# Three buffers for gathered rows and an earlier lead for gathers, in a mixture-of-experts layer

## The chip, the core and the metric

The kernel runs on one core of a Trainium2 chip. A core has five engines, each with its own instruction stream: TensorE (PE in the profile, with its weight loads apart as PEld), VectorE (DVE), ScalarE (ACT), GpSimd (POOL) and SyncE (SP). DMA transfers are issued by an engine into a queue and run beside the engines. The metric is the device time of one execution in microseconds (us); the figure given is the median of several runs.

## What is computed

One layer of a hybrid model over 1024 tokens of width 1024, in float32: a state-space mixer and a windowed attention in parallel, an output projection, a mixture of 32 experts, and a final norm. Only the expert stage matters here. In the reference it is (cut):

```
def hier_moe(h, w_group, b_group, w_expert, b_expert, w_gate, w_up, w_down):
    ...            # top-1 of 4 groups, then top-2 of its 8 experts; weights per token
    order = jnp.argsort(flat_e)
    ...            # assignments sorted by expert into blocks of 128, each of one expert
    x_buf = h_pad[tok_buf].reshape(n_blocks, MOE_BLOCK, d)
    def expert_block(args):
        xb, e = args
        return (jax.nn.silu(xb @ w_gate[e]) * (xb @ w_up[e])) @ w_down[e]
    y_buf = lax.map(expert_block, (x_buf, blk_e)).reshape(n_slots, d)
    out = jax.ops.segment_sum(y_buf.astype(f32) * w_buf[:, None], tok_buf, num_segments=n_tok + 1)
```

`w_gate` and `w_up` are 1024 x 512 for each expert, `w_down` is 512 x 1024: 6 MB of weights per expert, all of which must be read.

## The kernel before

**Blocks.** The expert stage (`moe`) walks 33 blocks, one for each place in a list of experts, and one more for the second part of the expert at place 13 (`MID`). The order is 0 to 13, then block 32 (`NE`), then 14 to 31. Fifteen places (`HALVES`: 3, 4, 6, 8, 10, 12, 14, 16, 18, 20, 22, 24, 27, 29, 31) and block 32 are half blocks, with up to 64 tokens; below they carry an h (block 10h). The others are full blocks of up to 128 tokens. An expert whose tokens don't fit is finished in `moe_rest`, a loop over overflow blocks near 990 us.

**One block.** A table in device memory, `tab`, holds for each block its token numbers, its output rows and its weights.
- `lst_load` brings a block's table entries into `lst` (DMAs on SP's queue, L1198: one for a full block, two for a half block, since the 64 entries are laid down twice). For a half block it then makes the half-row numbers `hrow` with one VectorE instruction (L1200): 64 tokens by two half rows of 512.
- `gather` issues an indirect DMA on POOL's queue that fetches the block's rows from `h2d` into `xe` (L1236 with `lst`, 128 x 1024; L1231 with `hrow`, 128 x 512, which fills half of the buffer only). There are two `xe` buffers, used in turn.
- `x_t` (L1306) or `half_x` (L1249) transposes the rows on PE into `pxe`; ScalarE and VectorE copy them out.
- `gu` (L1319) or `half_gu` (L1260) multiplies by the gate and up weights into `pgu`, the activation follows, and `down` (L1345) or `half_down` (L1284) multiplies by the down weights into `py`.
- `y_out` (L1351, tile `ye`) or `half_y` (L1289, `yeh`, in the same two buffers) weighs the result on VectorE.
- `y_add` (L1355) or `half_add` (L1293) issues an indirect DMA on POOL's queue that adds the rows of `ye` to `acc` in device memory.

**Weights.** 192 loads of 1 MB (tile `wf`, L1215, on SP's queue) go through 13 slots. For full blocks ScalarE (L179, `wh`) and VectorE (L180, `wl`) split them into a high and a low part; half blocks use them as they are.

**Order.** `schedule` lists the steps; behind the third quarter of block p's gate and up matmuls stands a step ("x", p), at which `x_ahead` transposes the next block, issues the gather of the block two behind that one, and has loaded the entries two blocks before the gather. The instructions of each engine are then put into a fixed order by a scheduler at build time, and every engine works through its order; POOL issues gathers and adds in one row, so an instruction that waits holds up all behind it.

Of the kernel before, what the change touches and what calls it, by code (L numbers as in the profile page):

```python
# [17 lines left out]
P = 128  # L18
# [7 lines left out]
NE = 32  # L26
# [12 lines left out]
OOB = 1 << 20  # L39

NR, NL, NW = 7, 6, 4

NCH = 6

# [80 lines left out]
class Kern:  # L125
# [1049 lines left out]

    def moe_bufs(self):
        nc = self.nc
        self.xe = [self.mp([D], "xe%d" % k) for k in range(2)]
        for t in self.xe:
            nc.gpsimd.memset(t, 0.0)  # L1180
        self.lst = self.mp([NE + 1, 4], "lst", 1, I32)
        self.hrow = self.mp([NE + 1], "hrow", 1, I32)
        self.EV = {}
# [5 lines left out]
    def lst_load(self, b):  # L1189


        nc = self.nc
        e = self.expert_at(MID if b == NE else b)
        r, n = P if b == NE else 0, H if self.half(b) else P
        tv = self.tab.rearrange("(e r) c -> e r c", e=NE)[:, r:r + n, :]
        src = tv[e] if isinstance(e, int) else tv[bass.ds(e, 1)].rearrange("o r c -> (o r) c")
        for p in range(0, P, n):
            nc.sync.dma_start(out=self.lst[p:p + n, b, :], in_=src)  # L1198
        if self.half(b):
            nc.vector.tensor_scalar(self.hrow[:, b:b + 1], self.lst[:, b, 0:1], 2.0, self.C[:, C_HALF:C_HALF + 1], op0=OP.mult, op1=OP.add)  # L1200

    def side(self):

# [25 lines left out]
    def gather(self, k, lst, b=None):  # L1229
        if b is not None and self.half(b):  # L1230
            self.nc.gpsimd.indirect_dma_start(  # L1231
                out=self.xe[k % 2][:, 0:D // 2], out_offset=None, in_=self.h2d.rearrange("t (a c) -> (t a) c", a=2),
                in_offset=bass.IndirectOffsetOnAxis(ap=self.hrow[:, b:b + 1], axis=0),
                bounds_check=2 * NT - 1, oob_is_err=False)
            return
        self.nc.gpsimd.indirect_dma_start(  # L1236
            out=self.xe[k % 2], out_offset=None, in_=self.h2d[:, :],
            in_offset=bass.IndirectOffsetOnAxis(ap=lst[:, 0:1], axis=0),
            bounds_check=NT - 1, oob_is_err=False)


    def half_x(self, k):

        nc = self.nc
        xv = self.xe[k % 2][:, 0:D // 2].rearrange("s (p i) -> s i p", i=4)
        xT = self.mp([4, P], "xT", 2, tag="xh", size=D)
        ps = self.bank([4, P], name="pxe")
        for i in range(4):
            nc.tensor.transpose(ps[:, i, :], xv[:, i, :], self.ident)  # L1249
        nc.scalar.copy(xT, ps)  # L1250
        return xT
# [45 lines left out]

    def x_t(self, e, out=None, ps=None):
        nc = self.nc
        xv = self.xe[e % 2].rearrange("s (a p i) -> s a i p", a=2, i=4)  # L1300
        xh, xl = out or (self.mp([8, P], "xh", 2, F32R), self.mp([8, P], "xl", 2, F32R))
        fixed = ps
        for h in range(2):
            ps = self.bank([4, P], name="pxe") if fixed is None else fixed
            for k in range(4):
                nc.tensor.transpose(ps[:, k, :], xv[:, h, k, :], self.ident)  # L1306
            s = slice(4 * h, 4 * h + 4)
            nc.scalar.copy(xh[:, s, :], ps)
            nc.vector.tensor_tensor(xl[:, s, :], ps, xh[:, s, :].bitcast(F32), OP.subtract)
        return xh, xl  # L1310
# [138 lines left out]
    def moe(self):  # L1449
        blocks = list(range(MID + 1)) + [NE] + list(range(MID + 1, NE))  # L1450
        at = lambda p: [p, NE] if p == MID else [p]
        X, A, T, Y, Z, G = {}, {}, {}, {}, {}, {}
        done = 0
        add = lambda b: self.half_add(Z.pop(b), b) if self.half(b) else self.y_add(Z.pop(b), self.lst[:, b, :])

        def x_ahead(p):

            nonlocal done
            for b in at(p):
                k = blocks.index(b)  # L1460
                X[b] = self.half_x(k) if self.half(b) else self.x_t(k)
                for i in range(done, min(k + 3, NE + 1)):
                    if 4 <= i + 2 < NE + 1:
                        self.lst_load(blocks[i + 2])
                    self.gather(i, self.lst[:, blocks[i], :], blocks[i])
                done = min(k + 3, NE + 1)

        for i in range(3):
            self.lst_load(i)
        for i in range(2):  # L1470
            self.gather(i, self.lst[:, i, :])
        self.g2 = self.mod_load(self.mp, 3, "g2")
        self.g2h = self.mp([512], "g2h")
        for n in range(2):
            self.nc.sync.dma_start(out=self.g2h[n * H:n * H + H], in_=self.modd[3][None, n * 512:n * 512 + 512].to_broadcast([H, 512]))
        self.counts()
        self.lst_load(3)
        done = 2
        x_ahead(0)
        for t in self.steps:  # L1480
            k, p = t[0], t[-1] if len(t) == 2 else t[1] if len(t) > 2 else None
            if k == "gu":
                if t[2] == 0:
                    for b in at(p):
                        G[b] = self.bank2(name="pgu")
                wg, wu = self.parts_for(p, (2 * t[2], 2 * t[2] + 1), (0, 0, 2, NW)[t[2]])
                for b in at(p):
                    if self.half(b):
                        self.half_gu(t[2], X[b], *((wg, wu) if self.half(p) else (wg[2], wu[2])), G[b])
                    else:  # L1490
                        self.gu(t[2], X[b], wg, wu, G[b])
            elif k == "act":
                for b in at(p):
                    A[b] = (self.half_act if self.half(b) else self.act)(G.pop(b))
            elif k == "x":
                if p + 1 < NE:
                    x_ahead(p + 1)
            elif k == "hT":
                for b in at(p):
                    T[b] = (self.half_h if self.half(b) else self.h_t)(A.pop(b))  # L1500
                    Y[b] = self.bank2(name="py")
            elif k == "down":
                w, = self.parts_for(p, (8 + t[2],), 0)
                for b in at(p):
                    if self.half(b):
                        self.half_down(T[b], w if self.half(p) else w[2], Y[b], t[2])
                    else:
                        self.down(T[b], w, Y[b], t[2])
            elif k == "y":
                for b in at(p):  # L1510
                    Z[b] = self.half_y(Y.pop(b), b) if self.half(b) else self.y_out(Y.pop(b), self.lst[:, b, :])
                    if p != REST - 1:
                        add(b)
            elif k == "rest":
                self.moe_rest()
                self.rested = True
                for b in list(Z):
                    add(b)
            elif k == "final":
                self.final()  # L1520
            elif k == "last":
                self.final_rows(Y.pop(p))
# [63 lines left out]
    def final(self):  # L1586

        nc = self.nc
        self.nf = self.mp([D], "nf", 2, tag="xl")
        nc.scalar.dma_start(out=self.nf, in_=self.a["norm_final"].to_broadcast([P, D]))  # L1590
        self.nfh, self.pair = self.mp([D // 2], "nfh", 2, tag="xh", size=D), self.mp([P], "pair")
        for n in range(2):
            nc.scalar.dma_start(out=self.nfh[n * H:n * H + H], in_=self.a["norm_final"][:, n * 512:n * 512 + 512].to_broadcast([H, 512]))

            nc.vector.tensor_tensor(self.pair[:, n * H:n * H + H], self.ident[:, 0:H], self.ident[:, H:P], OP.add)
        hr = self.mp([1], "hr", 1, I32)
        nc.vector.tensor_scalar(hr, self.lst[:, NE - 1, 1:2], 2.0, self.C[:, C_HALF:C_HALF + 1], op0=OP.mult, op1=OP.add)
        self.rowsy = self.mp([D // 2], "ya", 2, tag="xl", size=D)
        nc.gpsimd.indirect_dma_start(
            out=self.rowsy, out_offset=None, in_=self.acc.rearrange("t (a c) -> (t a) c", a=2),  # L1600
            in_offset=bass.IndirectOffsetOnAxis(ap=hr[:, 0:1], axis=0),
            bounds_check=2 * (NT + P) - 1, oob_is_err=False)
        ys = [self.mp([D], "yf", NW, tag=("wh", "wl")[b % 2]) for b in range(NBX)]
        for b in range(NBX):
            nc.sync.dma_start(out=ys[b], in_=self.acc[b * P:(b + 1) * P, :])
        self.ys = ys
# [165 lines left out]
```

## Time and profile before

| | us |
|---|---|
| median of 3 runs | 1357.1 (1354.55 to 1357.25) |
| profiled execution, time | 1359.11 |
| its span | 1357.3 |
| PE busy | 1167.5 (86%) |
| DVE, ACT, POOL busy | 829.9, 599.3, 337.4 |
| first gather of the expert stage issued | 693.45 |
| last add of the expert stage issued | 1316.70 |

The profile comes from one execution of its own, recorded by the hardware. A row of the timeline gives the start, the length, the engine, the source line, the operation, "out<-in" by tile names, the count of instructions in the row (x3) and, in brackets, how long the engine sat idle ahead of it and what released it. "issue" there means that it waited for nothing that the profile shows. Waits are listed as total us, times, longest us. A window's row gives the busy time of each engine, the granted PE clock (1.00 is full), the busy share of the 16 DMA engines (which can exceed 1 a little) and GB/s.

### The profile page before, as it was taken

The numbers are of one execution on the slowest core, as the hardware profiler recorded it, in microseconds if no ns is written. First come the engines' busy times: TensorE is split into PE (matmuls) and PEld (weight loads), VectorE is DVE, ScalarE is ACT, GpSimd is POOL, SyncE is SP. The second block draws the span as 40 slices with busy tenths as digits, with TensorE's granted clock in tenths as the row PEclk, the third lists the DMA queues.
The fourth block names the chain that finished last, engine by engine and source line by source line (L and its number), as shares of the span: only waits on it lengthen the run. The fifth ranks groups of instructions, "written<-read, shape, count | busy, mean of one in ns | idle before, by whom it ended". The sixth has DMA issues, their size and how long they took to land. (4 is left out here: it accounts for less than half of the span.)

```text
span 1357.3 us, 18757 instructions
## 1 busy us (share of the span) xinstructions
PE 1167.5 (86%) x6630; PEld 859.6 (63%) x6630; DVE 829.9 (61%) x1399; ACT 599.3 (44%) x1064; POOL 337.4 (25%) x290
## 2 busy tenths in 40 slices
PE   5799999888888999899938999697999968989981
PEld 2588778788876666687726666454556645566550
DVE  1688984788848877556678544353456535466533
ACT  4633322455367766433436434333244423354323
POOL 0340001577623444022331121111121211102110
PEclk9789999989888999999969899798999979989996
DMA  9755645766223300873467899999589999989846
GB/s 330 266 200 163 209 139 157 250 204 202 96 77 120 109 9 16 293 265 124 165 235 262 312 371 406 374 353 361 206 322 402 404 376 319 343 327 355 334 154 263
DMA packets 104512, 335.02 MB, mean 247 GB/s; under 512 B 19562, under 2 KB 37994, under 8 KB 79840
## 3 DMA queue, kind: packets, MB, share of 16 engines
q1 hardware_dynamic: 94672, 314.78, 62.4%
q0 software_dynamic: 9008, 17.10, 5.3%
q10 hardware_dynamic: 736, 1.92, 0.4%
q8 instruction: 53, 0.87, 0.3%
q14 instruction: 43, 0.35, 0.1%
HBM read 299.74 MB, written 43.43 MB: 253 GB/s over the span
## 5 line engine op out<-in xcount | busy, mean ns | idle before, releaser
L180 DVE TENSOR_TENSOR wl<-wf,wh 128x1024 fp32r<-128x1024 f32 x204 | 242.0, 1221 | 118.8 <-ACT wh L179 118.3
L179 ACT CAST wh<-wf 128x1024 fp32r<-128x1024 f32 x204 | 205.1, 1051 | 175.3 <-PE pgu L1319 140.2
L1260 PE MATMUL pgu<-wf,xT 128*64 128x256 f32 x1024 | 130.6, 386 | 0.4 <-DVE yeh L1289 0.4
L1319 PE MATMUL pgu<-wl,xh 128*128 128x512 f32 x272 | 95.3, 418 | 12.7 <-DVE wl L180 12.5
L1260 PEld LDWEIGHTS pgu<-wf,xT 128*64 128x64 f32 x1024 | 71.9, 137 | 47.9 <-issue 12.6
L1319 PE MATMUL pgu<-wh,xh 128*128 128x512 f32 x272 | 97.6, 432 | 4.4 <-ACT wh L179 4.4
L466 PE MATMUL pzq<-xw,hxh 128*128 128x256 f32 x512 | 100.2, 295 | 0.0
L768 POOL TENSOR_SCALAR p<-p,sst 128x640 f32<-128x640 f32 (+1 forms) x32 | 66.1, 2065 | 103.9 <-DVE sst L765 53.7
L1355 POOL DMA_INDIRECT acc<-ye,lst x17 | 33.5, 1972 | 234.4 <-DVE ye L1351 164.2
L1319 PE MATMUL pgu<-wh,xl 128*128 128x512 f32 x272 | 89.0, 407 | 0.0
L1345 PE MATMUL py<-wh,hT 128*128 128x512 f32 x272 | 81.9, 410 | 2.3 <-ACT hT L1337 2.3
L466 PEld LDWEIGHTS pzq<-xw,hxh 128*128 128x128 f32 x512 | 83.1, 197 | 1.0 <-issue 0.2
L347 PE MATMUL pxb<-hxh,xw 128*128 128x512 f32 x256 | 76.4, 397 | 0.0
L1319 PEld LDWEIGHTS pgu<-wl,xh 128*128 128x128 f32 x272 | 53.8, 198 | 32.6 <-DVE wl L180 20.2
L466 PE MATMUL pzq<-xw,hxl 128*128 128x256 f32 x256 | 74.3, 290 | 0.0
L1319 PEld LDWEIGHTS pgu<-wh,xh 128*128 128x128 f32 x272 | 52.0, 201 | 34.2 <-ACT wh L179 18.8
L1306 PE MATMUL pxe<-C,xe 128*128 128x128 f32 x136 | 26.5, 332 | 51.9 <-DMA xe<-h2d,lst 49.2
L1293 POOL DMA_INDIRECT acc<-yeh,hrow x15 | 32.8, 2185 | 153.8 <-DVE yeh L1289 136.9
L751 DVE TENSOR_REDUCE sst<-psc 128x1 f32<-128x640 f32 (+1 forms) x64 | 50.4, 789 | 29.7 <-PE psc L750 24.7
L1284 PE MATMUL py<-wf,hTh 128*64 128x512 f32 x256 | 64.1, 622 | 0.5 <-ACT hTh L1277 0.5
L1345 PEld LDWEIGHTS py<-wh,hT 128*128 128x128 f32 x272 | 50.3, 193 | 20.4 <-issue 5.3
L1319 PEld LDWEIGHTS pgu<-wh,xl 128*128 128x128 f32 x272 | 53.6, 197 | 14.3 <-issue 3.2
(352 smaller groups left out, 2528.6 us busy)
## 6 DMA issues: line engine op xcount, KB each, us to landing
wf<-in_w_gate SPq DMA_DIRECT2D x64, 1024.0 KB, 14.1
wf<-in_w_up SPq DMA_DIRECT2D x64, 1024.0 KB, 8.7
wf<-in_w_down SPq DMA_DIRECT2D x64, 1024.0 KB, 13.2
wa<-in_w_ada SPq DMA_DIRECT2D x48, 512.0 KB, 4.7
R<-csd SPq DMA_DIRECT2D x16, 512.0 KB, 4.7
xl<-xd SPq DMA_DIRECT2D x17, 256.0 KB, 3.4
xt<-in_x SPq DMA_DIRECT2D x8, 512.0 KB, 7.9
xf<-in_w_xbc SPq DMA_DIRECT2D x8, 512.0 KB, 4.3
```

The lines of the kernel that those rows point to most:

```text
L179: self.nc.scalar.copy(hi, src)
L180: (eng or self.nc.vector).tensor_tensor(lo, src, hi.bitcast(F32), OP.subtract)
L347: nc.tensor.matmul(px[s], w(wp, kc), self.hx(hp, kc, s, 512), start=st, stop=sp)
L466: nc.tensor.matmul(ps, self.hx(hp, kc, b // 4, P, (b % 4) * P), w(wp, kc), start=kc == 0 and hp + wp == 0, stop=kc == KC - 1 and hp == 1)
L751: v.tensor_reduce(mx, ps[:, o:512 + nl], AX.X, OP.max)
L768: (v if j % 2 else nc.gpsimd).tensor_scalar(p_, p_, den[:, j - i:j - i + 1], None, op0=OP.mult)
L1260: self.nc.tensor.matmul(pg[n * H:n * H + H, o:o + 256], xT[:, i0 + kk, a * H:a * H + H], w[:, kk * 512 + n * 256:kk * 512 + n * 256 + 256] ...
L1284: self.nc.tensor.matmul(py[n * H:n * H + H, 0:512], hT[:, i, a * H:a * H + H], w[:, n * 512:n * 512 + 512], start=f == 0, stop=f == 3)
L1293: self.nc.gpsimd.indirect_dma_start(out=self.acc.rearrange("t (a c) -> (t a) c", a=2), out_offset=bass.IndirectOffsetOnAxis(ap=self.hrow[: ...
L1319: nc.tensor.matmul(pg[:, n * 512:(n + 1) * 512], x[xp][:, k, :], w[wp][:, kk * 512:(kk + 1) * 512], start=k == 0 and xp + wp == 0, stop=k ...
L1345: nc.tensor.matmul(py[:, n * 512:(n + 1) * 512], hT[:, hp, f, :], wd[wp][:, n * 512:(n + 1) * 512], start=f == 0 and hp + wp == 0, stop=f ...
L1355: self.nc.gpsimd.indirect_dma_start(out=self.acc[:, :], out_offset=bass.IndirectOffsetOnAxis(ap=lst[:, 0:1], axis=0), in_=y, in_offset=Non ...
```

## The change

A third `xe` buffer is added (`NX`), with its memset. `x_ahead` for the block at place k now issues gathers up to place k+3 (it was k+2), makes half-row numbers up to place k+4, and loads table entries up to place k+6. At the start three gathers and seven blocks' entries are issued (two and four before). Making half-row numbers is split from `lst_load` into `half_rows`. The small tile `pair`, used at the end, shares the buffers of `hT`. Core of the diff (`% 2` became `% len(self.xe)` in `gather`, `half_x` and `x_t` too):

```diff
+NX, TABLE_AHEAD = 3, 3
...
-        self.xe = [self.mp([D], "xe%d" % k) for k in range(2)]
+        self.xe = [self.mp([D], "xe%d" % k) for k in range(NX)]
...
+    def half_rows(self, b):
         if self.half(b):
-            nc.vector.tensor_scalar(self.hrow[:, b:b + 1], ...)
+            self.nc.vector.tensor_scalar(self.hrow[:, b:b + 1], ...)
...
-        done = 0
+        done = rows = tabs = 0
...
         def x_ahead(p):
-            nonlocal done
             for b in at(p):
                 k = blocks.index(b)
                 X[b] = self.half_x(k) if self.half(b) else self.x_t(k)
-                for i in range(done, min(k + 3, NE + 1)):
-                    if 4 <= i + 2 < NE + 1:
-                        self.lst_load(blocks[i + 2])
-                    self.gather(i, self.lst[:, blocks[i], :], blocks[i])
-                done = min(k + 3, NE + 1)
-
-        for i in range(3):
-            self.lst_load(i)
-        for i in range(2):
-            self.gather(i, self.lst[:, i, :])
+                rows_to(k + NX + 1)
+                gather_to(k + NX + 1)
+                rows_to(k + NX + 2)
+                tables_to(k + NX + 1 + TABLE_AHEAD)
+
+        def gather_to(n):
+            nonlocal done
+            for i in range(done, min(n, NE + 1)):
+                self.gather(i, self.lst[:, blocks[i], :], blocks[i])
+                done = i + 1
...
+        def tables_to(n):
+            nonlocal tabs
+            for i in range(tabs, min(n, NE + 1)):
+                self.lst_load(blocks[i])
+                tabs = i + 1
+
+        tables_to(FIXED)
+        gather_to(FIXED)
...
-        self.lst_load(3)
-        done = 2
+        tables_to(NX + 1 + TABLE_AHEAD)
         x_ahead(0)
...
-        self.nfh, self.pair = self.mp([D // 2], "nfh", 2, tag="xh", size=D), self.mp([P], "pair")
+        self.nfh, self.pair = self.mp([D // 2], "nfh", 2, tag="xh", size=D), self.mp([P], "pair", 2, tag="hT", size=D)
```

`rows_to` is the same loop over `half_rows`; `FIXED` is 3. In the new kernel the lines of the block functions stand 2 to 4 further down: gathers are L1240 and L1235, transposes L1310 and L1253, adds L1359 and L1297, gate and up matmuls L1323 and L1264, `yeh` L1293.

What this does to the orders is shown at two places. First POOL's order before, from the gather of block 7 to that of block 11. `xe_6889` and `xe_6890` are the two buffers; the gathers are of blocks 7, 8h, 9, 10h and 11, and the adds of blocks 4h, 5, 6h and 7:

```order
L1236 DMA xe_6890<-h2d,lst 128x1024
L1293 DMA acc<-yeh,hrow 2304x512
L1231 DMA xe_6889<-h2d,hrow 128x512
L1355 DMA acc<-ye,lst 1152x1024
L1236 DMA xe_6890<-h2d,lst 128x1024
L1231 DMA xe_6889<-h2d,hrow 128x512
L1293 DMA acc<-yeh,hrow 2304x512
L1355 DMA acc<-ye,lst 1152x1024
L1236 DMA xe_6890<-h2d,lst 128x1024
```

And now, from the gather of block 9 to that of block 13, with `xe_6891` as the third buffer; the gathers are of blocks 9, 10h, 11, 12h and 13, and the adds of blocks 5, 6h and 7:

```order
L1240 DMA xe_6889<-h2d,lst 128x1024
L1359 DMA acc<-ye,lst 1152x1024
L1235 DMA xe_6890<-h2d,hrow 128x512
L1240 DMA xe_6891<-h2d,lst 128x1024
L1297 DMA acc<-yeh,hrow 2304x512
L1235 DMA xe_6889<-h2d,hrow 128x512
L1359 DMA acc<-ye,lst 1152x1024
L1240 DMA xe_6890<-h2d,lst 128x1024
```

Block 11's gather stood behind block 7's add and now stands behind block 5's, with block 10h's gather between; it is block 13's gather that follows block 7's add now.

Second, PE around the transposes of blocks 10h and 11, in the stretch of block 9's down matmuls (`py`) and of block 10h's gate and up matmuls (`pgu<-wf,xT`). Before:

```order
L1260 MATMUL pgu<-wf,xT 64x256
L1249 MATMUL pxe<-C,xe_6889 128x128 x4
L1345 MATMUL py<-wl,hT 128x512 x2
...
L1345 MATMUL py<-wh,hT 128x512 x2
L1260 MATMUL pgu<-wf,xT 64x256 x16
L1275 MATMUL phT<-C,hgh 128x128 x2
L1306 MATMUL pxe<-C,xe_6890 128x128 x4
L1319 MATMUL pgu<-wh,xh 128x512
L1306 MATMUL pxe<-C,xe_6890 128x128 x4
```

And now:

```order
L1264 MATMUL pgu<-wf,xT 64x256
L1253 MATMUL pxe<-C,xe_6890 128x128 x4
L1310 MATMUL pxe<-C,xe_6891 128x128
L1349 MATMUL py<-wl,hT 128x512 x2
...
L1349 MATMUL py<-wh,hT 128x512 x2
L1264 MATMUL pgu<-wf,xT 64x256 x2
L1310 MATMUL pxe<-C,xe_6891 128x128 x2
L1264 MATMUL pgu<-wf,xT 64x256 x14
L1310 MATMUL pxe<-C,xe_6891 128x128
L1279 MATMUL phT<-C,hgh 128x128 x2
L1310 MATMUL pxe<-C,xe_6891 128x128 x3
```

The eight transposes of block 11 stood behind block 10h's activation; the first now stands right behind block 10h's own transposes, and the others are spread over the down matmuls of block 9 and the rest of block 10h.

More of the change, by code (lines that the diff above doesn't have):

```diff
@@ L1198, in lst_load @@
             nc.sync.dma_start(out=self.lst[p:p + n, b, :], in_=src)
+    def half_rows(self, b):
         if self.half(b):
-            nc.vector.tensor_scalar(self.hrow[:, b:b + 1], self.lst[:, b, 0:1], 2.0, self.C[:, C_HALF:C_HALF + 1], op0=OP.mult, op1=OP.add)
+            self.nc.vector.tensor_scalar(self.hrow[:, b:b + 1], self.lst[:, b, 0:1], 2.0, self.C[:, C_HALF:C_HALF + 1], op0=OP.mult, op1=OP.add)
     def side(self):
@@ L1231, in gather @@
             self.nc.gpsimd.indirect_dma_start(
-                out=self.xe[k % 2][:, 0:D // 2], out_offset=None, in_=self.h2d.rearrange("t (a c) -> (t a) c", a=2),
+                out=self.xe[k % len(self.xe)][:, 0:D // 2], out_offset=None, in_=self.h2d.rearrange("t (a c) -> (t a) c", a=2),
                 in_offset=bass.IndirectOffsetOnAxis(ap=self.hrow[:, b:b + 1], axis=0),
@@ L1236, in gather @@
         self.nc.gpsimd.indirect_dma_start(
-            out=self.xe[k % 2], out_offset=None, in_=self.h2d[:, :],
+            out=self.xe[k % len(self.xe)], out_offset=None, in_=self.h2d[:, :],
             in_offset=bass.IndirectOffsetOnAxis(ap=lst[:, 0:1], axis=0),
@@ L1244, in half_x @@
         nc = self.nc
-        xv = self.xe[k % 2][:, 0:D // 2].rearrange("s (p i) -> s i p", i=4)
+        xv = self.xe[k % len(self.xe)][:, 0:D // 2].rearrange("s (p i) -> s i p", i=4)
         xT = self.mp([4, P], "xT", 2, tag="xh", size=D)
@@ L1299, in x_t @@
         nc = self.nc
-        xv = self.xe[e % 2].rearrange("s (a p i) -> s a i p", a=2, i=4)
+        xv = self.xe[e % len(self.xe)].rearrange("s (a p i) -> s a i p", a=2, i=4)
         xh, xl = out or (self.mp([8, P], "xh", 2, F32R), self.mp([8, P], "xl", 2, F32R))
@@ L1461, in x_ahead, with rows_to @@
                 X[b] = self.half_x(k) if self.half(b) else self.x_t(k)
-                for i in range(done, min(k + 3, NE + 1)):
-                    if 4 <= i + 2 < NE + 1:
-                        self.lst_load(blocks[i + 2])
-                    self.gather(i, self.lst[:, blocks[i], :], blocks[i])
-                done = min(k + 3, NE + 1)
-        for i in range(3):
-            self.lst_load(i)
-        for i in range(2):
-            self.gather(i, self.lst[:, i, :])
+                rows_to(k + NX + 1)
[7 more added lines that the diff above has]
+                done = i + 1
+        def rows_to(n):
+            nonlocal rows
+            for i in range(rows, min(n, NE + 1)):
+                self.half_rows(blocks[i])
+                rows = i + 1
+        def tables_to(n):
[5 more added lines that the diff above has]
+        gather_to(FIXED)
         self.g2 = self.mod_load(self.mp, 3, "g2")
```

## The prediction

> **What bounds the kernel now.** I read the page's busy shares first, then what TensorE (PE) waits for, then PE's timeline at each of those waits, and last POOL's timeline just before them, since POOL issues the gathers.
>
> ```profile
> PE 1167.5 (86%) x6630; PEld 859.6 (63%) x6630; DVE 829.9 (61%) x1399; ACT 599.3 (44%) x1064; POOL 337.4 (25%) x290
> ...
> PE pxe L1306 <- DMA xe<-h2d,lst: 49.2, 7, 17.2
> PE pgu L1319 <- DVE wl L180: 12.5, 12, 1.9
> PE pxe L1249 <- DMA xe<-h2d,hrow: 11.1, 2, 6.5
> ...
> 700.33 0.89 PE L1306 MATMUL pxe<-C,xe 128*128 128x128 f32 x3 [17.17 <-DMA xe<-h2d,lst]
> 749.18 0.89 PE L1306 MATMUL pxe<-C,xe 128*128 128x128 f32 x3 [4.91 <-DMA xe<-h2d,lst]
> 870.47 0.89 PE L1306 MATMUL pxe<-C,xe 128*128 128x128 f32 x3 [10.74 <-DMA xe<-h2d,lst]
> 948.64 0.92 PE L1249 MATMUL pxe<-C,xe 128*128 128x128 f32 x3 [6.46 <-DMA xe<-h2d,hrow]
> 1108.49 0.67 PE L1306 MATMUL pxe<-C,xe 128*128 128x128 f32 x2 [11.03 <-DMA xe<-h2d,lst]
> 1149.90 0.91 PE L1306 MATMUL pxe<-C,xe 128*128 128x128 f32 x3 [4.28 <-DMA xe<-h2d,lst]
> 1191.18 1.10 PE L1249 MATMUL pxe<-C,xe 128*128 128x128 f32 x4 [4.67 <-DMA xe<-h2d,hrow]
> ```
>
> PE is busy 86% of the span. In the expert stage its largest waits are for gathered rows: 49.2 us (full blocks) and 11.1 us (half blocks) in total. The timeline places them: the first, 17.17 us, is the stage's very first gather, which nothing in the change brings forward; six of 4.28 to 11.03 us follow. Why are those gathers late?
>
> ```profile
> 835.62 1.03 POOL L1231 DMA_INDIRECT xe<-h2d,hrow  x1 [10.73 <-PE pxe L1249]
> ...
> 856.28 1.58 POOL L1355 DMA_INDIRECT acc<-ye,lst  x1 [17.70 <-DVE ye L1351]
> 858.16 1.07 POOL L1236 DMA_INDIRECT xe<-h2d,lst  x1 [0.31 <-PE pgu L1260]
> ...
> 1117.54 1.04 POOL L1231 DMA_INDIRECT xe<-h2d,hrow  x1 [21.05 <-issue]
> ...
> DMA to landing us min/median/max: 3.3/7.7/12.9
> ```
>
> The last row is for tile xe: a gather takes 3.3 to 12.9 us to land. The gather of block 11 (858.16) stands on POOL right behind block 7's add (856.28), and POOL sat 17.70 us until VectorE had that add's ye. 858.16 + about 12 us of landing is the 870.47 at which PE goes on. So the gather is late by its place in POOL's order, not by its transfer. Block 10h's gather at 835.62, by contrast, waited for its buffer, and the one at 1117.54 for something that the profile does not name (in POOL's order and in its code the half-row number is the one input left).
>
> **The change, part by part.** *Gathers three blocks ahead, into three buffers.* The number of gathers (33), adds and table entries stays. In the new order block 11's gather stands behind the adds up to block 5's and gather 10; it goes into the buffer that block 8h left at 835.62 less 0.3, the end that gather 10 waited for above. It then lands at 835.6 + 7.7 to 12.9 = 843 to 848.5. I walked POOL's whole new order in this way, with the old trace's times for transposes, ye and landings: every gather starts 12 to 75 us earlier and lands at least 13 us before its old need. Block 11 is the exception, because PE now takes its first transpose right behind block 10h's:
>
> ```profile
> 848.91 0.75 PE L1249 MATMUL pxe<-C,xe 128*128 128x128 f32 x4
> ```
>
> That is 849.7 against 848.5 at worst by the row, up to 3 us of wait if the transfer is slower; I take 1. The removable waits are 49.2 + 11.1 - 17.2 = 43.1 us: -42.1 with that one taken off. What is late next on PE is the L1319 wait for split weights, 12.5 us in 12 pieces.
>
> *The clock after each stall.* Columns of the windows: length, then busy us of PE, PEld, DVE, ACT and POOL with counts, granted clock, DMA share, GB/s.
>
> ```profile
> 749.20:753.20 4.00, 4.00 (x12) 3.25 (x13) 0.00 (x0) 0.00 (x0) 0.00 (x0) 0.50 0.99 374
> 870.50:874.50 4.00, 4.00 (x14) 3.49 (x15) 0.00 (x0) 0.00 (x0) 0.00 (x0) 0.53 0.88 365
> ...
> 1191.20:1195.20 4.00, 4.00 (x12) 3.32 (x13) 0.94 (x1) 0.00 (x0) 0.00 (x0) 0.51 0.73 273
> ...
> 873.08 1.05 PE L1319 MATMUL pgu<-wl,xh 128*128 128x512 f32 x2
> 879.38 0.63 PE L1319 MATMUL pgu<-wh,xh 128*128 128x512 f32 x2
> ```
>
> For about 4 us behind each of the six stalls (first two and last shown) the granted clock is 0.50 to 0.53; two matmuls take 1.05 us there and 0.63 later. 4 x (1 - 0.63/1.05) = 1.6 us lost each, 6 x 1.6 = 9.6. By the clock alone it would be 2.0 each, 12. I take -9.6, the pair of rows being the same work.
>
> *A third memset.*
>
> ```profile
> 691.18 1.84 POOL L1180 MEMSET xe<- 128x1024 f32 x2 [1.27 <-DMA tab<-pay,rows]
> 693.45 1.05 POOL L1236 DMA_INDIRECT xe<-h2d,lst  x1 [0.43 <-DMA lst<-tab]
> ```
>
> 1.84/2 = 0.92 us more ahead of the first gather, for which PE waits in the open: +0.9 (0.5 if half is taken by the 0.43 that POOL waits there for the table). The third early gather is issued behind the first, on its queue: 0.
>
> *Table entries and half-row numbers earlier.* SP issues three more entry DMAs (blocks 5 and 6h) before a weight load:
>
> ```profile
> 696.23 3.13 SPq L1198 DMA_DIRECT2D lst<-tab  x4
> 699.47 0.53 SPq L1215 DMA_DIRECT2D wf<-in_w_gate  x1
> ...
> SPq L1215 <- DVE wl L180: 145.1, 45, 13.1
> ```
>
> 3 x 3.13/4 = 2.3 us, once. Afterwards each pair of blocks brings the same entries as before. SP waits 145.1 us in its weight loads for slots that the splits free, so the loads go when slots come free, not when SP does: 0 (at most +2.3). Half-row numbers are one 0.2 us VectorE instruction each at nearly the same places, but now one block ahead of the gather; the 21.05 us at 1117.54 cost PE nothing by themselves, and what they cost behind them goes with the 43.1. The two `pair` operations in another buffer: 0, VectorE idles near them.
>
> *Adds behind more gathers.* POOL's order now puts gathers in front of some adds, and a gather may wait for transposes. By the walk the adds start at most 2.5 us later, worst at block 17's:
>
> ```profile
> 1059.41 2.31 POOL L1355 DMA_INDIRECT acc<-ye,lst  x1 [13.46 <-DMA wf<-in_w_up]
> ...
> 1093.54 1.58 POOL L1355 DMA_INDIRECT acc<-ye,lst  x1 [15.22 <-DVE ye L1351]
> ...
> DMA to landing us min/median/max: 3.5/9.0/11.7
> ```
>
> The last row is for tile acc. 1059.41 + 2.5 + 2.3 + 11.7 = 1075.9, and the ye that overwrites the buffer two blocks later is written from about 1092.0 (1093.54 less 0.3 and a ye of 1.3). 16 us are left: 0.
>
> *Can the weights keep up?* Without stalls the same bytes must come in less time.
>
> ```profile
> 1000.00:1090.00 90.00, 89.38 (x474) 59.46 (x473) 51.16 (x54) 41.85 (x53) 20.36 (x12) 1.00 1.02 405
> 760.00:960.00 200.00, 175.08 (x937) 111.80 (x937) 96.27 (x103) 74.11 (x96) 35.45 (x22) 0.94 0.95 361
> 760.00:1280.00 520.00, 461.15 (x2409) 299.96 (x2410) 263.86 (x278) 205.47 (x261) 89.09 (x56) 0.95 0.93 349
> ```
>
> From 760 to 1280 us 349 x 520 = 181.5 MB move. The waits in it are 43.1 - 4.9 = 38.2 us and five restarts 8.0, so 473.8 us would be left. At the 405 GB/s of 1000 to 1090, where PE ran without a break, the bytes need 448 us. By DMA share 0.93 x 520 / 1.02 = 474, just what is left. At 361/0.95 = 380 GB/s they need 478. So DMA becomes nearly as tight as PE. I take +4 (478 against 474); the ends are 0 and, if no more than the 361 GB/s of the 200 us window holds over a long stretch, 181.5/0.361 = 503, +29. The row of 90 unbroken us is nearest to the new state, hence 4.
>
> A rule that speaks against the change: the Trainium skill, page "Perfetto Trace Analysis", section "Identifying the Most-Contended Engine", holds that matmul busy time is no measure of TensorE's headroom, and that weight-load busy and, for DMA, memory utilization are. By it PE is not the bound in 1000 to 1090 (59.46 of 90, 66%). The Trainium skill, same page, section "Roofline", gives 358 GB/s as a core's share of memory; by that figure the bytes need 507 us and the sum would end near 1339, an estimate from that page. The same section lets a core that runs alone go to about 435 GB/s, and the 405 GB/s here, on a lone core, agree with that.
>
> Sum: -42.1 - 9.6 + 0.9 + 4 = -46.8. The profiled execution took 1359.1 us (span 1357.3), so 1312.3; the median of the runs is 1357.1, 2.0 lower: 1310. What follows the last block (final adds, norm, output) is untouched.
>
> **The rivals.** *A. The weights bind.* The same stalls go, but PE then waits on L1319 for splits and their loads. For it: DMA share 0.93 to 1.02 already, with the stalls in. Against: 90 us at 405 GB/s with 89.38 of them busy. Cost 12 to 29 us instead of 4: 1318 to 1335, around 1326. The 358 GB/s of the Trainium skill, page "Perfetto Trace Analysis", section "Roofline", would put it just past its upper end.
>
> *B. A gather holds up an add.* If the gather of half block 8 waits for all readers of its buffer, and not for those of the half it overwrites, it stands on POOL until block 5's second-half transposes, and block 1's add stands behind it:
>
> ```profile
> 763.80 2.34 POOL L1355 DMA_INDIRECT acc<-ye,lst  x1 [15.00 <-DVE ye L1351]
> 789.57 0.75 DVE L1289 SCALAR_TENSOR_TENSOR yeh<-py,lst,g2h 128x512 f32<-128x512 f32 x1 [5.89 <-PE py L1284]
> 790.33 0.75 PE L1306 MATMUL pxe<-C,xe 128*128 128x128 f32 x4
> ...
> 722.09 1.56 POOL L1231 DMA_INDIRECT xe<-h2d,hrow  x1 [10.59 <-PE pxe L1306]
> 724.09 0.27 PE L1306 MATMUL pxe<-C,xe 128*128 128x128 f32 x1
> ```
>
> Issue at 791.1 + 1.1 + 0.4, landing about 11 later: 804, while yeh of block 3 wants the ye buffer at 789.57. 14 us late, some 12 on PE and 1.6 of clock: 1324. Against it: at 722.09 a half gather went while its buffer's last transposes (724.09) were still to come.
>
> *C. It doesn't do what it says.* Were block 11's gather still behind block 7's add, nothing would move: 1357. The order speaks against it.
>
> *D. Slower.* PE without pauses is granted less clock. 461.15 busy us lie in 760 to 1280; the loss outweighs 46.8 where the mean clock falls below 461.15/(461.15 + 46.8) = 0.91 from 1.00. At 0.88 it costs 63 and gives 1373. The 1.00 through 90 unbroken us speaks against it.
>
> **How the numbers follow.** The forecast, with its own range 1301 (-43.1 - 12 + 0.5 = -54.6, and 1.5 us of spread between runs) to 1318, has 0.62; A 0.20, B 0.09, C 0.05, D 0.04. The range 1301 to 1331 leaves out C, D, a third of A (0.07) and 0.03 of the forecast: 0.19. 0.2% is 2.7 us, about what a measurement of this kernel can tell from no change; faster 0.91 (the forecast, A, B), same 0.05 (C), slower 0.04 (D).
>
> **What would show it.** The xe waits at L1310 and L1253 fall from 60.3 to about 18 us, the first one left; POOL's gathers name transposes or the preceding issue as their release, not ye. Windows of 40 us in the stage show PE at 39 or more and the clock at 1.00 but for the overflow check near 990. DMA stands at 1.00 to 1.02 and 385 to 405 GB/s. A shows as L1323 waits well above 12.5 us, B as a yeh waiting for acc near 790, D as a clock under 0.95 in unbroken windows. I am wrong if PE's new waits exceed 15 us.

## The result, and the profile after

The changed kernel takes 1312.3 us (median of 4 runs, 1309.4 to 1316.1) against 1355.9 for the kernel before on the same chip: ratio 0.968, 95% interval 0.965 to 0.971. Two later comparisons gave 0.9645 (0.960 to 0.969) and 0.965 (0.961 to 0.969). Forecast were 1310 us and a range from 1301 to 1331.

What PE waited for, after (total us, times, longest us); this answers to the first rows shown of before:

```profile
PE pxe L1310 <- DMA xe<-h2d,lst: 18.5, 1, 18.5
PE pgu L1323 <- DVE wl L182: 12.7, 14, 1.8
...
PE pgu L1323 <- ACT wh L181: 6.6, 9, 1.4
...
PE pxe L1310 <- ACT xT L1254: 3.9, 6, 1.0
```

Of the 60.3 us of waits for gathered rows one is left, the stage's first gather, and no wait for a half gather. POOL's timeline from the add of block 5 to the gather of block 13 (start, length, engine, line, operation, idle before it and its releaser):

```profile
808.21 2.31 POOL L1359 DMA_INDIRECT acc<-ye,lst  x1 [13.50 <-DVE ye L1355]
810.83 1.08 POOL L1235 DMA_INDIRECT xe<-h2d,hrow  x1 [0.31 <-issue]
822.62 1.03 POOL L1240 DMA_INDIRECT xe<-h2d,lst  x1 [10.71 <-PE pxe L1253]
823.96 1.61 POOL L1297 DMA_INDIRECT acc<-yeh,hrow  x1 [0.30 <-issue]
825.88 1.38 POOL L1235 DMA_INDIRECT xe<-h2d,hrow  x1 [0.31 <-issue]
843.57 1.59 POOL L1359 DMA_INDIRECT acc<-ye,lst  x1 [16.31 <-DMA wf<-in_w_up]
845.47 1.04 POOL L1240 DMA_INDIRECT xe<-h2d,lst  x1 [0.31 <-issue]
```

Block 11's gather (822.62) now waits for the transposes that free its buffer, and stands 21 us ahead of the add of block 7 (843.57) behind which it stood before. It is block 13's gather that follows that add. POOL still waits 13 to 16 us ahead of an add (for the second one the profile names a weight load as the last release, not ye); nothing that PE needs soon is queued behind it.

The stage in one window each, from PE's first transpose (700.33 before, 694.30 after) to the transposes of block 31 (1271.3, 1225.4). Columns: length; busy us of PE, PEld, DVE, ACT and POOL with counts; granted clock; DMA share; GB/s. The first row is of before, the second of after:

```profile
700.33:1271.30 570.97, 503.01 (x2569) 334.14 (x2569) 302.36 (x342) 235.06 (x296) 98.27 (x61) 0.94 0.90 337
```
```profile
694.30:1225.40 531.10, 503.09 (x2569) 329.72 (x2569) 303.79 (x342) 236.63 (x298) 97.73 (x60) 0.97 0.95 364
```

The stage is 39.9 us shorter. PE's busy time in it is the same to 0.1 us, and its idle time fell from 68.0 to 28.0. The span fell by 46.7 (1357.3 to 1310.6): 39.9 here, 6.0 ahead of the stage's first transpose, 0.8 behind it. The 6.0 can't be credited to the change, as the third experiment below shows.

### The profile page after: what moved, and what is told of

Same layout as the page of the kernel before. It is cut to its first block, busy times and chain, and to the rows that moved or that the text cites. A ratio compares the mean times of both kernels' runs of the same rounds, so it can differ in the third digit from the quotient of the medians.

```text
span 1310.6 us, 18757 instructions
## 1 busy us (share of the span) xinstructions
PE 1163.3 (89%) x6630; PEld 851.8 (65%) x6630; DVE 827.3 (63%) x1399; ACT 599.0 (46%) x1064; POOL 338.9 (26%) x291
## 5 line engine op out<-in xcount | busy, mean ns | idle before, releaser
L1264 PE MATMUL pgu<-wf,xT 128*64 128x256 f32 x1024 | 133.2, 390 | 0.4 <-DVE yeh L1293 0.4
L1323 PE MATMUL pgu<-wl,xh 128*128 128x512 f32 x272 | 96.7, 419 | 13.5 <-DVE wl L182 12.7
L1264 PEld LDWEIGHTS pgu<-wf,xT 128*64 128x64 f32 x1024 | 72.4, 138 | 48.7 <-issue 13.4
L1323 PE MATMUL pgu<-wh,xh 128*128 128x512 f32 x272 | 95.9, 427 | 6.6 <-ACT wh L181 6.6
L1323 PE MATMUL pgu<-wh,xl 128*128 128x512 f32 x272 | 88.5, 405 | 0.0
L1359 POOL DMA_INDIRECT acc<-ye,lst x17 | 32.0, 1885 | 210.4 <-DVE ye L1355 115.6
L1323 PEld LDWEIGHTS pgu<-wl,xh 128*128 128x128 f32 x272 | 53.3, 196 | 36.1 <-DVE wl L182 22.3
L1323 PEld LDWEIGHTS pgu<-wh,xh 128*128 128x128 f32 x272 | 50.7, 196 | 38.6 <-ACT wh L181 22.3
L1297 POOL DMA_INDIRECT acc<-yeh,hrow x15 | 31.8, 2118 | 138.3 <-DVE yeh L1293 122.3
L1323 PEld LDWEIGHTS pgu<-wh,xl 128*128 128x128 f32 x272 | 53.3, 196 | 13.9 <-issue 3.2
L756 ACT ACTIVATE p<-psc,sst 128x640 f32<-128x640 f32 (+1 forms) x64 | 49.3, 771 | 15.6 <-DVE sst L767 7.6
```

The lines of the kernel that those rows point to most:

```text
L756: nc.scalar.activation(p_[:, :NCX + nl], ps[:, o:512 + nl], AF.Exp, bias=nm, scale=0.125, accum_out=den)
L1264: self.nc.tensor.matmul(pg[n * H:n * H + H, o:o + 256], xT[:, i0 + kk, a * H:a * H + H], w[:, kk * 512 + n * 256:kk * 512 + n * 256 + 256] ...
L1323: nc.tensor.matmul(pg[:, n * 512:(n + 1) * 512], x[xp][:, k, :], w[wp][:, kk * 512:(kk + 1) * 512], start=k == 0 and xp + wp == 0, stop=k ...
L1359: self.nc.gpsimd.indirect_dma_start(out=self.acc[:, :], out_offset=bass.IndirectOffsetOnAxis(ap=lst[:, 0:1], axis=0), in_=y, in_offset=Non ...
```

## The experiments

My theory: the gathers were late because of their place in POOL's order, behind adds that waited for ye, and the change mends that order. Its rivals: the third buffer itself (a gather could not start for want of one), the longer lead, or the half-row numbers. The kernels of each set ran beside the kernel before on one chip.

**1. Two buffers, all else early.** `NX` is 2, so gathers lead by two blocks as before; tables and half-row numbers come as in the change.

```diff
-NX, TABLE_AHEAD = 3, 3
+NX, TABLE_AHEAD = 2, 3
...
-        gather_to(FIXED)
+        gather_to(NX)
```

> Two xe buffers and gathers two blocks ahead as before; table entries and half-row numbers issued as early as in the change. Theory 1 (the late gathers came from POOL's order, in which they stood behind adds; the new order here puts block 11's gather ahead of block 7's add without a third buffer): the big waits go, and about 8 to 14 us of short ones stay, at blocks 5, 11, 23 and 28, where the gather waits for the buffer: 1318 to 1328 us. Theory 2 (the third buffer is what frees the gathers): most waits stay, 1340 to 1357 us.

Measured: 1328.9 us, ratio 0.978 (0.973 to 0.982). A little above the expected band, and far from the rival's: 25 of the 46 us that the change brought in this set (third experiment) come without the third buffer. Behind the first, three xe waits of 11.5 us in all were left, the largest at block 28:

```profile
1163.59 1.10 PE L1310 MATMUL pxe<-C,xe 128*128 128x128 f32 x4 [8.32 <-DMA xe<-h2d,lst]
...
1149.77 1.59 POOL L1359 DMA_INDIRECT acc<-ye,lst  x1 [14.86 <-DMA wf<-in_w_up]
1151.66 1.06 POOL L1240 DMA_INDIRECT xe<-h2d,lst  x1 [0.30 <-issue]
```

It is the old pattern: its gather (1151.66) comes right behind an add that POOL waited 14.86 us to issue.

**2. Three buffers, one part of the lead taken back each.** The first keeps the gathers at two blocks ahead. The second keeps them at three, and makes table entries and half-row numbers together, two blocks ahead of the gather, as before. (The diffs here and in the fourth experiment are cut to `x_ahead`.)

```diff
-                rows_to(k + NX + 1)
-                gather_to(k + NX + 1)
-                rows_to(k + NX + 2)
-                tables_to(k + NX + 1 + TABLE_AHEAD)
+                rows_to(k + LEAD + 1)          # LEAD = 2
+                gather_to(k + LEAD + 1)
+                rows_to(k + LEAD + 2)
+                tables_to(k + LEAD + 1 + TABLE_AHEAD)
```

> Three xe buffers, but gathers two blocks ahead as before; table entries and half-row numbers three and one blocks ahead of them as in the change. Theory 1 (POOL's order, and the buffer free early): 4 us of xe wait at most, 1310 to 1318 us. Theory 3 (the gather's lead of three blocks is what counts): most waits stay, 1335 to 1357 us.

```diff
+                for i in range(done, min(k + NX + 1, NE + 1)):
+                    tables_to(i + 3)
+                    rows_to(i + 3)
+                    gather_to(i + 1)
```

> Three xe buffers and gathers three blocks ahead as in the change, but table entries and half-row numbers made together two blocks ahead of their gather, as before. Theory 1: a gather three blocks ahead has time to wait for its half-row numbers, 4 us of xe wait at most, 1310 to 1318 us. Theory 4 (late half-row numbers, as at 1117.54 us before, held POOL's queue): POOL waits for them again and half or more of the stalls return, 1330 to 1350 us.

Measured: 1320.7 us, ratio 0.974 (0.970 to 0.978), and 1321.9 us, 0.974 (0.971 to 0.978). Both lie some us above my band, and between two buffers and the change. In both one late gather is left, again that of block 28, 8.4 and 8.5 us; this is its row in the second:

```profile
1157.98 0.46 PE L1310 MATMUL pxe<-C,xe 128*128 128x128 f32 x1 [8.53 <-DMA xe<-h2d,lst]
```

Neither the lead alone nor the half-row numbers explain the gain, and the parts overlap. The second kernel, with the buffer and the lead but the entries no earlier ahead of their gather than before, has 32 of the 46 us. Added last, the lead is worth 13 us and the early entries and half-row numbers 14; the buffer is worth 8 beside two buffers with all else early, and there the intervals overlap. What a third buffer would bring to the old order no run shows. In POOL's order of these three kernels, as in the change, block 11's gather stands ahead of block 7's add. Only with third buffer, lead and early tables together does the gather of block 28 come ahead of the adds of blocks 22 and 23.

**3. The changed kernel again.**

> The changed kernel once more. The time ahead of the expert stage was 7 us shorter in its profile than in that of the kernel before, though all five engines' orders are the same up to there. If that is a difference from run to run, the start of the stage (first table entry at 691.1 before, 684.0 after) moves by some us again and the median stays within 1309 to 1316 us; if it came with the change, it stands at 684 within 1 us again.

Measured: 1308.0 us, ratio 0.9645 (0.960 to 0.969). The stage's first transpose started at 700.5 us here, against 694.3 in the first profile, and at 703.1 in a third (below): the time ahead of the stage moves by 9 us between runs of one program. The 6.0 us of the first profile are therefore not shown to come from the change.

**4. Which of the early things matters: tables or half-row numbers.** Both have two buffers and gathers two blocks ahead.

```diff
 # tables early, half-row numbers at their load
+                for i in range(done, min(k + 3, NE + 1)):
+                    gather_to(i + 1)
+                    tables_to(i + 4)
+                    rows_to(i + 4)
...
 # half-row numbers one block ahead of the gather, tables as before
+                for i in range(done, min(k + 3, NE + 1)):
+                    tables_to(i + 3)
+                    rows_to(i + 1)
+                    gather_to(i + 1)
+                    rows_to(i + 2)
```

> Of the change only one thing: table entries are loaded three blocks ahead of the gather and behind the gather in the program, not two and ahead of it. Two xe buffers, gathers two blocks ahead, half-row numbers made right at their load. POOL's order built from this has the gathers of 11, 12h, 23 and 24h ahead of the adds of 7, 8, 19 and 20. Theory 1 (POOL's order is the cause, and the scheduler sets it by when it thinks that the table entries arrive): as with two buffers and all early, 1320 to 1330 us, four xe waits of 2 to 9 us behind the first. Theory 5 (the half-row numbers had to be parted from their load): as the kernel before, 1345 to 1357 us.

> Of the change only the other thing: half-row numbers made one block ahead of their gather and apart from the load; two xe buffers, gathers and table entries two blocks ahead as before. POOL's order is that of the kernel before. Theory 1: no change, within 0.4% of the kernel before, 43 us of xe waits behind the first. Theory 5 (late half-row numbers made the gathers late): 10 us or more faster.

Measured: 1335.2 us, ratio 0.980 (0.972 to 0.988), for the tables alone, and 1358.1 us, ratio 1.001 (0.997 to 1.004), for the half-row numbers alone. The first is some 2% faster, with single runs from 1322.9 to 1340.5 and so partly above its band; behind the first, five xe waits of 17 us in all were left, and the one at block 11 came down to 2.5. The second changed nothing, and block 11's gather stood where it had stood, right behind an add that POOL waited 17.72 us to issue:

```profile
858.71 1.58 POOL L1359 DMA_INDIRECT acc<-ye,lst  x1 [17.72 <-DVE ye L1355]
860.59 1.07 POOL L1240 DMA_INDIRECT xe<-h2d,lst  x1 [0.31 <-PE pgu L1264]
...
872.89 0.46 PE L1310 MATMUL pxe<-C,xe 128*128 128x128 f32 x1 [10.74 <-DMA xe<-h2d,lst]
```

The second is no test of earlier half-row numbers, though, because VectorE still ran all but one of those instructions in their old places. The one for block 24h ran at 1118.57 us, 1.0 us before the gather that waited 20.36 us for a release without a name; in the kernel before it ran at 1116.55, 1.0 us before the gather at 1117.54. That fits the prediction's reading of this wait. Theory 5 fails by the first kernel, which gains with the half-row numbers at their load, and by other rows. In the kernel before, PE did not wait for block 24h, and each of the six late gathers stood right behind an add that POOL had waited 13.8 to 17.7 us to issue. Block 11's pair is shown in the prediction; these are the pairs of blocks 5, 14h, 23, 25 and 27h:

```profile
737.44 2.36 POOL L1355 DMA_INDIRECT acc<-ye,lst  x1 [13.79 <-DVE ye L1351]
740.10 1.39 POOL L1236 DMA_INDIRECT xe<-h2d,lst  x1 [0.31 <-issue]
...
938.25 1.57 POOL L1355 DMA_INDIRECT acc<-ye,lst  x1 [16.60 <-DVE hrow L1200]
940.12 1.07 POOL L1231 DMA_INDIRECT xe<-h2d,hrow  x1 [0.30 <-PE pgu L1260]
...
1093.54 1.58 POOL L1355 DMA_INDIRECT acc<-ye,lst  x1 [15.22 <-DVE ye L1351]
1095.43 1.06 POOL L1236 DMA_INDIRECT xe<-h2d,lst  x1 [0.30 <-issue]
...
1141.21 1.57 POOL L1355 DMA_INDIRECT acc<-ye,lst  x1 [16.60 <-DVE ye L1351]
1143.09 1.07 POOL L1236 DMA_INDIRECT xe<-h2d,lst  x1 [0.30 <-PE pgu L1260]
...
1182.23 1.59 POOL L1355 DMA_INDIRECT acc<-ye,lst  x1 [16.59 <-DVE hrow L1200]
1184.12 1.08 POOL L1231 DMA_INDIRECT xe<-h2d,hrow  x1 [0.30 <-issue]
```

Where a half-row number is named, VectorE had ended it 0.1 us behind the ye (938.08 and 937.96 at the first), so it cost almost nothing.

So a piece that looks small, table entries loaded one block earlier, gives 22 us, about half of the gain of the change (44 to 46 us), though its interval is wide. On the chip these entries had not been late. In the kernel before, SP issued those of block 11 at 824.67, and its gather went 33 us later, at 858.16:

```profile
824.67 0.33 SPq L1198 DMA_DIRECT2D lst<-tab  x1
```

What the earlier load changed is the order that was built. On POOL, with the half-row numbers alone (the adds of blocks 6h and 7, the gathers of 10h, 11 and 12h):

```order
L1235 DMA xe_6889<-h2d,hrow 128x512
L1297 DMA acc<-yeh,hrow 2304x512
L1359 DMA acc<-ye,lst 1152x1024
L1240 DMA xe_6890<-h2d,lst 128x1024
L1235 DMA xe_6889<-h2d,hrow 128x512
```

and with the tables alone:

```order
L1235 DMA xe_6889<-h2d,hrow 128x512
L1297 DMA acc<-yeh,hrow 2304x512
L1240 DMA xe_6890<-h2d,lst 128x1024
L1359 DMA acc<-ye,lst 1152x1024
L1235 DMA xe_6889<-h2d,hrow 128x512
```

Block 11's gather and block 7's add have changed places. That the scheduler does so because it reckons with a late arrival of the entries is my reading of the two orders. The order and its price on the chip are shown.

**5. Does the supply of weights bind?** First try: one more transfer of 0.5 or 1 MB a block from a weight array to memory that nothing reads.

```diff
+        self.extra = self.dram.tile([NE + 1, P, 1024], F32, name="extra")   # 2048 in the second
...
+                self.nc.sync.dma_start(out=self.extra[k], in_=self.w_src(k % FIXED, 0)[:, 0:1024])
```

> The changed kernel, with one more transfer of 0.5 MB for each of 32 blocks, from a weight array to memory of its own that nothing reads, on SP's queue: 16.8 MB more in a stage that moves about 193 MB. Forecast's theory (the DMA engines have about 5% left, 407 GB/s at most against 364 used): the stage needs 210/0.407 = 516 us, below the 525 to 531 it takes, so 0 to +8 us. Rival A (the loads bind already): each byte costs its time, +41 us at 407 GB/s.

> The same with 1 MB for each block, 33.6 MB more. Forecast's theory: now the loads bind, 227/0.407 = 557 us against 525 to 531, so +26 to +33 us. Rival A: +82 us.

Measured: 1314.3 us, ratio 0.968 (0.962 to 0.974), and 1323.9 us, 0.974 (0.969 to 0.980). This says nothing of the stage, which took 529.0 us in the profile of the second. The transfers depend on nothing, and the tile view of the second shows them issued between 63.9 and 413.7 us, long before it:

```profile
L1470 SPq DMA_DIRECT2D extra<-in_w_gate x33: 494/495/2773, 63.9 to 413.7; - x33
```

So bytes were tied to the stage by storing ye (512 KB, or 256 KB for a half block) of 30 blocks to unused memory, once or three times, behind its add on POOL's queue:

```diff
                     if p != REST - 1:
+                        z = Z[b]
                         add(b)
+                        for q in range(n):                                   # n is 1, then 3
+                            self.nc.gpsimd.dma_start(out=self.extra[n * b + q][...], in_=z)
```

> The extra loads of the last runs were issued between 64 and 414 us, ahead of the expert stage, and so tested nothing there. Here each ye or yeh is also stored once to memory that nothing reads, on POOL's queue right behind its add, which ties the bytes to the stage: 12.5 MB more than 193. Forecast's theory (407 GB/s at most, 364 used): 205/0.407 = 505 us, below the 525 to 531 that the stage takes; 0 to +5 us against the changed kernel on this chip. Rival A (the DMA engines bind already): +31 us.

> The same with three stores, 37.5 MB more. Forecast's theory: now DMA binds, 231/0.407 = 566 us against 525 to 531, so +30 to +41 us, with PE waiting for split weights. Rival A: +92 us. If it is far below +30, DMA had more left than the windows show.

Measured, with the changed kernel at 1312.4 us (ratio 0.965, 0.961 to 0.969) beside them: 1318.5 us, ratio 0.970 (0.965 to 0.975), and 1370.6 us, 1.009 (1.007 to 1.012). By the bytes of the profiles (347.1 and 371.2 MB, against 335.0) 12.1 and 36.2 MB were added, a little less than the expectations say. Of 12.1 MB, which at 405 GB/s are 30 us, 6 came through, and the two intervals overlap. Of 36.2 MB, 89 us at that rate, 58 came through, above the expected 41 and far below rival A's 92. The stage with three stores, and what PE waits for in that kernel:

```profile
695.50:1277.10 581.60, 514.50 (x2569) 335.42 (x2569) 304.66 (x341) 236.95 (x296) 137.20 (x141) 0.94 0.97 380
```
```profile
PE pgu L1323 <- ACT wh L181: 30.4, 19, 4.7
PE pxe L1310 <- DMA xe<-h2d,lst: 18.8, 1, 18.8
PE pxe L1310 <- SPq L1570: 16.4, 1, 16.4
```

Now PE does wait for weights (30.4 us for the first part of the split, 6.6 in the changed kernel), and 16.4 us at the overflow check, against 2.1. ScalarE's splits waited 120 us for loads, against 2.4 to 6.1 us in three profiles of the changed kernel. PE's busy time is 514.5 us, 11 to 19 more than there. Without the extra bytes the loads are not the bound, but the room is small: an estimate from these two runs is 24 to 31 us' worth, 10 to 13 MB of 193, taking all that came through as the price of the bytes.

**6. The memsets, and the changed kernel a third time.**

```diff
-            nc.gpsimd.memset(t, 0.0)
+            nc.vector.memset(t, 0.0)
```

> The changed kernel with the three memsets of xe on VectorE, so that POOL issues the first gather without them. By the changed kernel's trace the gather then waits for the table entry alone, some 1.5 to 2.8 us earlier: 1 to 3 us faster than the changed kernel, and the first xe wait shorter by that. Rival: the memsets cost nothing where they stood, because the first gather waits for the table entry in any case: no change.

> The changed kernel a third time, beside the three above on one chip. PE's busy time in the stage was 503.1 us in one profile and 495.4 in the next, of the same program with the same waits. If the clock after short waits varies from run to run, it lies anywhere from 495 to 504 here; if the first profile was an outlier, at 495 to 497.

Measured: 1310.8 us, ratio 0.964 (0.960 to 0.968), beside the changed kernel's 1312.4, 0.965 (0.961 to 0.969). The intervals lie on each other, so no gain is shown. The trace says why there could be little: the memset waits for the table's write wherever it is issued, and POOL's gather now waits for VectorE. It goes 2.04 us behind the table's write (696.12 to 698.16), against 2.94 in the third profile of the change: 0.9 us earlier, less than the 1.5 expected at least. The first xe wait was 17.0 us, which lies among those of the kernels with two memsets (16.8 to 20.3).

What `after_third` was for, PE's busy time in the stage, came out at 501.4 us, within its band for a clock that varies from run to run; the next section takes it up.

```profile
696.12 0.91 DVE L1182 MEMSET xe<- 128x1024 f32 x1 [8.77 <-DMA tab<-pay,rows]
...
698.16 1.05 POOL L1240 DMA_INDIRECT xe<-h2d,lst  x1 [5.96 <-DVE xe L1182]
```

## Why the prediction was right, and where its terms were not

**Gathered rows: -42.1 forecast, -43.2 measured.** All six stalls and the two shorter ones are gone (idle time of PE before its transposes: 32.0 + 11.1 us behind the first wait before, 0 after). The 1 us kept back for block 11 was not needed. The reason given, the place in POOL's order, held: with two buffers and the order mended, 25 of the 46 us are there, and with two buffers and the old order none. The third buffer with its longer lead is worth the rest, 21 us in that set of runs (1328.9 against 1308.0).

**The clock after a stall: -9.6 forecast, between +0.1 and -7.6 measured.** This is the step that failed in size. The half-clock spells behind the six stalls are gone, but others came. The stage of the changed kernel in its second and third profile, one row each:

```profile
700.50:1225.50 525.00, 495.41 (x2569) 325.67 (x2569) 303.74 (x341) 236.59 (x298) 96.38 (x60) 0.99 0.95 367
```
```profile
703.07:1233.89 530.82, 501.37 (x2568) 328.68 (x2568) 303.78 (x341) 236.60 (x298) 97.09 (x60) 0.98 0.94 364
```

PE needs 495.4, 501.4 and 503.1 us for the same instructions, against 503.0 in the kernel before: -7.6, -1.6 and +0.1, a mean of -3.0. The kernel with the half-row numbers alone, which has the old order on POOL, gives 502.0, so the profile before is not an outlier. The forecast took away spells behind long waits, and did not see that short waits close together can make spells too. Two places, first in the first profile, then in the second:

```profile
847.12 0.39 PE L1310 MATMUL pxe<-C,xe 128*128 128x128 f32 x1 [0.96 <-ACT xT L1254]
...
847.12:851.12 4.00, 3.24 (x10) 1.98 (x11) 3.07 (x3) 4.00 (x5) 0.00 (x0) 0.78 1.02 362
922.28:926.28 4.00, 3.53 (x12) 1.27 (x14) 0.00 (x0) 3.46 (x5) 0.00 (x0) 0.77 0.93 296
```
```profile
853.36 0.39 PE L1310 MATMUL pxe<-C,xe 128*128 128x128 f32 x1 [0.96 <-ACT xT L1254]
...
853.36:857.36 4.00, 2.75 (x12) 1.77 (x13) 3.07 (x3) 4.00 (x5) 0.00 (x0) 1.00 1.02 370
926.41:930.41 4.00, 3.54 (x16) 1.37 (x18) 0.00 (x0) 3.46 (x5) 0.00 (x0) 1.00 0.99 311
```

Behind the same wait of 0.96 us, with one of 0.72 us soon after it in both runs, the clock fell in one run (0.78, and 0.50 from 850 to 852 us) and not in the other. In the second pair of windows, behind waits of 1.43 and 0.46 us in both runs, 12 matmuls ran in one run and 16 in the other.

The record of the granted clock that is kept with each trace shows how this comes about. The clock is 1.00 or 0.50 and changes only on a grid of 3.41 us, which is one for the whole stage: each spell of half clock in it lasts 3.41 us or a whole multiple. Apart from the spell in which the stage begins, the changed kernel spent 6.8, 20.5 and 23.9 us of the stage at half clock in the profiles with 495.4, 501.4 and 503.1 us, so each us of it cost about 0.45 us of PE time. Whether a spell follows goes with PE's work in the grid's window before it. In the three profiles, 437 such windows ran at full clock. All 13 in which PE was busy for at most 1.90 us were followed by half clock, and of the 424 with 1.99 us or more one was. The window of the first profile in which the waits of 0.96 and 0.72 us lie, and the two windows of the second in which they lie:

```profile
845.92:849.33 3.41, 1.73 (x12) 1.03 (x8) 1.71 (x3) 3.12 (x6) 0.59 (x1) 1.00 1.02 382
```
```profile
851.55:854.96 3.41, 2.30 (x15) 1.27 (x11) 1.09 (x2) 2.51 (x5) 1.04 (x1) 1.00 1.02 410
854.96:858.37 3.41, 2.31 (x9) 1.62 (x10) 3.41 (x4) 2.40 (x3) 0.00 (x0) 1.00 1.04 361
```

In one run both waits fall into one window and leave PE 1.73 us of work in it; in the other they are divided between two. The Trainium skill, page "TensorE: Matmul & The Clock Gate", section "Part 1: The HAM clock gate (the "warmup" mystery)", tells of an activity window of about 3.4 us that runs free of the program, so that the same program meets it at another phase in each run. The records agree with that. They differ from that section where it lets the clock fall after an idle window: here windows with up to 1.90 us of PE work were enough. Even the profile with the fewest spells gives -7.6 and not -9.6; what makes the rest is not shown.

**The memset: +0.9 forecast.** POOL's row grew from 1.84 to 2.73 us:

```profile
684.08 2.73 POOL L1182 MEMSET xe<- 128x1024 f32 x3 [1.53 <-DMA tab<-pay,rows]
```

From the table's write to the first gather it takes 2.27 us before (691.18 to 693.45) and 2.89, 2.88 and 2.94 us in the three profiles of the change. So the third memset delays the gather by 0.6 to 0.7 us, between the forecast's 0.9 and the 0.5 it gave as the lower value. What that costs PE can't be told apart: the first wait was 18.5, 19.1 and 20.0 us in these three profiles, and between 16.8 and 20.3 in four with two memsets.

**Supply and short waits: +4 forecast, +3.2 to +4.8 measured, for a reason that was forecast only in part.** Forecast was PE waiting for late weights. PE's idle time in the stage apart from the gathers went from 24.8 to 28.0, 29.6 and 29.5 us. Its waits for split weights did grow, from 14.4 to 16.5, 18.7 and 18.6 us. But the loads were hardly late: ScalarE's splits waited 2.4 to 6.1 us for them, and 92 to 103 us for PE's matmuls. What else delays the splits is not shown.

A second term was not forecast. The waits `pxe <- xT` grew from 0.5 to 3.9 us, while `phT <- hgh` fell by as much, from 5.7 to 2.4. The transposes of a full block now stand right behind those of the half block ahead, and wait until ScalarE has copied those out. ScalarE's copy in turn stands behind an activation that waits for the matmuls of another block:

```profile
846.21 0.38 ACT L1270 ACTIVATE sgh<-pgu 128x256 f32<-128x256 f32 x1 [8.92 <-PE pgu L1264]
846.49 0.58 ACT L1254 COPY xT<-pxe 128x512 f32<-128x512 f32 x1
```

These are the transposes of blocks 10h and 11. The matmuls among which they stand are block 7's down and block 8h's gate and up, and not those of 9 and 10h, as the text ahead of the prediction has it: block 7's add follows at 843.57. That the new order puts the two sets of transposes together was to be seen ahead of the prediction, and I did not price it. Rival A is refuted as the state of the changed kernel, though its point is near.

**B, C and D** did not come. No yeh waits near 790, the order does what it says, and the clock in a long stretch with hardly a break is 1.00, with the DMA share at the 1.02 of before:

```profile
1000.00:1080.00 80.00, 78.47 (x424) 51.22 (x423) 46.16 (x48) 36.82 (x48) 17.26 (x12) 1.00 1.02 401
```

Two of the signs named in the forecast did not come. In windows of 40 us from 720 to 1200 us PE was busy for 35.8 to 40.0 us, and not for 39 or more in each, and the clock was not 1.00 everywhere but at the overflow check.

**The sum.** By the terms measured, -43.2 - 3.0 + 4.2 (means of three profiles) make -42.0 in the stage; the three profiles gave -39.9, -46.0 and -40.1, and the medians of the three comparisons -43.6, -46.2 and -45.5. The forecast's -46.8 was right by its largest term. Its clock term was 6.6 too large, and runs differ by about that. That the first pair of profiles differs by 46.7, almost the forecast's sum, is luck: 6.0 of it lie ahead of the stage.

## What to carry to other kernels

On a queue that works in order, ask of each late transfer what stands ahead of it, before giving it another buffer: here a gather without any wait of its own stood behind an add, and loading its index one block earlier moved it and gave about half of the gain. When an edit is meant to move an instruction, look in the built order whether it moved. When a change takes away long waits, look for the short ones that its new order makes. And before resting on a supply that runs at its limit, add bytes that are tied to the stage, and check in the trace that they went there.

## What was not expected of the hardware

One and the same program took 495 to 503 us of PE time in one stage, with nearly equal waits. The granted clock fell for 3.41 us at a time, behind windows in which short waits left PE at most 1.90 us of work in 3.41, and where the windows lay differed from run to run. The part of the kernel ahead of the stage also ended 9 us apart in three runs of one program (694.3 to 703.1 at the first transpose).
